# The output projection of a hybrid mLSTM/S5 block as seven block products instead of a full product, with its weight differences built on the way

## The chip, the cores and the metric

The kernel runs on one core of one Trainium2 chip. The metric is the device time of one execution in microseconds; lower is better.

## The reference

A decoder block on x of 1024 x 1024 (sequence by width) in float32. What matters here is its frame and its end:

```python
xn = rmsnorm(x, norm_pre_g)
u_a, z_a, o_a, i_a, f_a, u_b, z_b, g_pre = split(xn @ w_in)
y_a = mlstm_branch(u_a, z_a, o_a, i_a + b_i, f_a + b_f, ...) @ w_a_out   # 4 heads, chunks of 128
y_b = s5_branch(u_b, z_b, ...) @ w_b_out                                 # width 512
g = sigmoid(g_pre)                                                       # 2048 gates per row
merged = g[:, :1024] * y_a + g[:, 1024:] * y_b
out = x + rmsnorm(merged @ w_o, norm_post_g)                             # w_o is 1024 x 1024
```

## The kernel before, in words

**Arithmetic.** Every float32 matrix product is made of three matmuls. `dot3` (L181 to L184) multiplies high half by high half (L182), high by low (L183) and low by high (L184). So each operand is split first: the high half is a copy on ScalarE (L142 for weights), the low half is the difference to it on VectorE or GpSimd (L144 for weights). Helper `tt` (L505) is an elementwise operation of VectorE; many rows bear its line.

**Engines and queues.** The program order is the order of each engine; nothing is reordered. Every DMA, load or store, is issued on SyncE's queue (SP in the profile) in program order, and where a DMA has to wait (for data, for a buffer, for an earlier DMA), SyncE waits and all later DMAs stand behind it. `store` (L82) puts a store on the list `pending`, and `tick`, which `run` calls ahead of every unit of work, issues what stands there. `run` also issues the loads of the next `look[0]` units ahead. Matmul results go to PSUM: three banks named `pp` and five named `pm`.

**Weights.** A plan (L231 to L254) lists weight tiles in order of use. `take` and `pump` load the raw tile `wr` (L124) and split it into `wh` and `wl` some time ahead; `wp` has two buffers of each.

**Stages.** Norm and transposes of x; the gates (written to DRAM as `t1_d` and `t2_d`); the S5 branch; then the stage around the change, "the yb stage": first 8 units of the gated unit `glu_unit`, then 16 of `yb_unit`, which make the gated y_b. Unit n of these 16 multiplies 4 row tiles of K by 512 columns (12 matmuls) into the next of the five `pm` banks; VectorE (L844) combines the bank with a gate tile `aux` (128x512, six buffers, loaded from `t2_d` at L820 three units ahead, as `look[0]` is 3), and the result goes to `gb_d`, 256 KB, at the next tick. Then the four mLSTM heads follow. They start with `o_unit`, one for each of the 8 row tiles: 24 matmuls into the next of the three `pp` banks, 264 columns wide for the first head since the 8 gate columns i and f come along. VectorE adds the bias tile `bif` to these 8 (`gall`, L505), which together with ScalarE's read frees the bank. `bif` is loaded by two small DMAs, L879 and L880, which stand in SyncE's order behind the last `gb_d` store of the yb stage. After the heads comes the merge: `mg_unit` multiplies the last K tiles of `w_a_out`, applies the gates, adds the part of y_b and splits the result to `mh` (ScalarE, L1439) and `ml` (GpSimd, L1440).

**Output projection.** `wo_unit` (L1445 on) runs over 4 blocks of 256 columns and 8 row tiles: 8 tiles of K times 3 matmuls of 256 columns. ScalarE squares the bank with a running sum (L1460), VectorE multiplies it by the norm's gains `gpo`. In the last block GpSimd makes the row's factor `fs` from the sums (L1467, L1468), and `finish` (L1474) multiplies two halves by it, adds x and stores them.

Of the kernel before, what the change touches and what calls it, by code (L numbers as in the profile page):

```python
# [36 lines left out]
def hybrid_block(ctx, tc, x, norm_pre_g, w_in, conv_w, conv_b, w_q, w_k, w_v, b_i, b_f, head_g,  # L37
# [799 lines left out]
    def yb_unit(i, m, hf):  # L837
        if m == 0 and hf == 0:
            cur["yb"] = take(("yb", i))
        ct = 4 * i + m  # L840
# [3 lines left out]
        V.scalar_tensor_tensor(t2, t2, 1.0, o, op0=ALU.add, op1=ALU.mult)  # L844
# [570 lines left out]
    mh, ml = {}, {}

    def mg_pre(ct, hf):
        rs = slice(ct * P, (ct + 1) * P)
# [4 lines left out]
        maux[ct, hf] = (t1, pr, None)

    def mg_unit(ct, hf):
        if "ya3" not in cur:
# [12 lines left out]
        A.activation(mh[ct, hf], t1, AF.Copy)  # L1439
        defer(lambda: PL.tensor_tensor(ml[ct, hf], t1, mh[ct, hf].bitcast(F32), op=ALU.subtract))  # L1440
# [4 lines left out]
    def wo_unit(i, t):  # L1445
        if t == 0:
            cur["wo", i] = take(("wo", i), i > 0)
        if i == 0:
# [11 lines left out]
        A.activation(jk, o[:, :256], AF.Square, scale=1.0 / 32.0, accum_out=sso[:, t, i:i + 1])  # L1460
# [4 lines left out]
        if i == 3:
            s = fp.tile([P, 1], F32, tag="fs", bufs=4, name="fs")
            PL.tensor_tensor(s, sso[:, t, 3:4], sso[:, t, 4:5], op=ALU.add)  # L1467
            PL.tensor_tensor(s, s, halfm[:, 0:1], op=ALU.pow)  # L1468
# [74 lines left out]
```

## Time and profile before

| | us |
|---|---|
| median of 3 runs (lowest to highest) | 987.84 (987.65 to 988.62) |
| profiled execution, whole | 987.63 |
| its span in the profile | 985.9 |
| TensorE busy (5644 matmuls) | 972.8 |
| VectorE, ScalarE, GpSimd busy | 621.9, 352.9, 207.1 |
| the 16 units of the yb stage on TensorE | 339.6 to 383.2 |
| the output projection's last matmul starts at | 979.6 |

The span is what the profiler saw from the first to the last instruction; the execution's own time is 1.7 us longer. Rows of the timeline give start, length, engine, line, operation, output and inputs, shapes and, in brackets, how long the engine had stood still and who released it. PE is TensorE's matmuls, DVE is VectorE, ACT ScalarE, POOL GpSimd, SPq the DMAs that SyncE issues. A matmul's stated length (0.39 us for 512 columns) is longer than the distance to the next one (0.23 us), as they overlap. The granted clock is 0.999 over the span.

### The profile page before, as it was taken

To read this page: it belongs to the slowest core of one execution; us is meant where nothing else is said; L and a number is where in the kernel's file an instruction comes from. 1 tells how busy PE (TensorE), PEld (TensorE's weight loads), DVE (VectorE), ACT (ScalarE), POOL (GpSimd) and SP (SyncE) were. 2 spreads that over 40 slices of the span, in tenths; PEclk is the share of its full clock that TensorE was granted. 3 is DMA by queue.
4 is the path that set the end of the run, shared out by engine and by line. 5 is a ranking of instruction groups with operands and counts; after the bars stand their busy time and mean duration, and the time that the engine had idled before them with its cause. 6 is when DMAs were issued, how large, how long until landed. Compare 5 with 4: busy or idle time off the path is not lost.

```text
span 985.9 us, 15233 instructions
## 1 busy us (share of the span) xinstructions
PE 972.8 (99%) x5644; PEld 840.9 (85%) x5644; DVE 621.9 (63%) x1397; ACT 352.9 (36%) x697; POOL 207.1 (21%) x215
## 2 busy tenths in 40 slices
PE   9999999999999999999999999998999999999997
PEld 7888888888887889978998898888988888879997
DVE  5437968879644752444686677747775888664225
ACT  7413132231314421224544445434543452233211
POOL 3013122111112000013111321223222311462002
PEclk9999999999999999999999999999999999999999
DMA  7454323423434566115344254335437895772504
GB/s 257 109 159 150 96 89 99 111 57 110 110 97 166 186 216 229 59 68 148 97 134 152 82 178 124 134 97 177 133 117 226 281 302 191 243 249 90 193 1 172
DMA packets 113722, 145.17 MB, mean 147 GB/s; under 512 B 18888, under 2 KB 71280, under 8 KB 113648
## 3 DMA queue, kind: packets, MB, share of 16 engines
q1 hardware_dynamic: 113648, 144.21, 46.0%
q8 instruction: 44, 0.72, 0.3%
q14 instruction: 30, 0.25, 0.1%
HBM read 98.79 MB, written 45.38 MB: 146 GB/s over the span
## 4 chain that ended last, share of the span: by engine, by line
PE 88%; issue 3%; POOL 3%; DVE 2%; DMA 2%; ACT 1%; SPq 0%; DVEq 0%; POOLq 0%; ACTq 0%
PE pp L182 24%; PE pp L183 23%; PE pp L184 23%; PE pm L184 4%; PE pm L182 4%; PE pm L183 4%; PE pm L1151 1%; POOL wl L144 1%; PE pm L727 1%; PE pm L768 1%; PE pm L767 1%; PE pm L1074 1%; DMA so_d<-sow 1%; POOL ml L1440 1%; POOL t2k L1270 1%
## 5 line engine op out<-in xcount | busy, mean ns | idle before, releaser
L182 PE MATMUL pp<-xh,wh 128*128 128x512 f32 x768 | 306.9, 400 | 0.0
L183 PE MATMUL pp<-xl,wh 128*128 128x512 f32 x768 | 303.8, 396 | 0.0
L184 PE MATMUL pp<-xh,wl 128*128 128x512 f32 x768 | 303.8, 396 | 0.0
L182 PEld LDWEIGHTS pp<-xh,wh 128*128 128x128 f32 x768 | 144.4, 188 | 35.1 <-ACT wt L691 0.8
L184 PEld LDWEIGHTS pp<-xh,wl 128*128 128x128 f32 x768 | 144.4, 188 | 34.6
L183 PEld LDWEIGHTS pp<-xl,wh 128*128 128x128 f32 x768 | 144.5, 188 | 32.4 <-DVE xl L295 0.3
L144 POOL TENSOR_TENSOR wl<-wr,wh 128x1024 fp32r<-128x1024 f32 (+1 forms) x25 | 61.6, 2482 | 229.1 <-ACT wh L142 229.1
L142 ACT ACTIVATE wh<-wr 128x1024 fp32r<-128x1024 f32 (+2 forms) x74 | 71.0, 1006 | 46.5 <-PE pm L183 30.6
L184 PE MATMUL pp<-wh,ml 128*128 128x256 f32 x256 | 72.6, 284 | 1.3 <-POOL ml L1440 1.3
L144 DVE TENSOR_TENSOR wl<-wr,wh 128x1024 fp32r<-128x1024 f32 (+2 forms) x49 | 55.9, 1172 | 27.7 <-ACT wh L142 23.2
L182 PE MATMUL pp<-wh,xh 128*128 128x256 f32 (+1 forms) x256 | 72.3, 282 | 0.6 <-ACT sow L902 0.6
L183 PE MATMUL pp<-wl,mh 128*128 128x256 f32 x256 | 72.5, 283 | 0.0
L182 PE MATMUL pp<-wh,mh 128*128 128x256 f32 x256 | 71.9, 281 | 0.0
L184 PE MATMUL pp<-wh,xl 128*128 128x256 f32 (+1 forms) x256 | 71.8, 281 | 0.0
L183 PE MATMUL pp<-wl,xh 128*128 128x256 f32 (+1 forms) x256 | 71.8, 280 | 0.0
L308 ACT ACTIVATE tg<-pp 128x512 f32<-128x512 f32 x32 | 19.2, 598 | 127.4 <-PE pp L184 89.4
L1048 POOL TENSOR_TENSOR hll<-t2k,hlh 128x512 fp32r<-128x512 f32 x16 | 21.1, 1319 | 182.7 <-ACT hlh L1047 106.0
L184 PEld LDWEIGHTS pp<-wh,ml 128*128 128x128 f32 x256 | 48.1, 188 | 1.7 <-POOL ml L1440 1.7
L182 PEld LDWEIGHTS pp<-wh,mh 128*128 128x128 f32 x256 | 48.7, 190 | 0.5 <-ACT mh L1439 0.4
L182 PEld LDWEIGHTS pp<-wh,xh 128*128 128x128 f32 x256 | 48.1, 188 | 1.2 <-ACT sow L902 1.0
L183 PEld LDWEIGHTS pp<-wl,xh 128*128 128x128 f32 x256 | 48.2, 188 | 0.2
L184 PEld LDWEIGHTS pp<-wh,xl 128*128 128x128 f32 x256 | 48.1, 188 | 0.0
(412 smaller groups left out, 1810.0 us busy)
## 6 DMA issues: line engine op xcount, KB each, us to landing
wr<-in_w_in_dram SPq DMA_DIRECT2D x48, 512.0 KB
t_d<-tg SPq DMA_DIRECT2D x32, 256.0 KB
xt<-in_x_dram SPq DMA_DIRECT2D x8, 512.0 KB
aux<-t_d SPq DMA_DIRECT2D x16, 256.0 KB
gb_d<-aux SPq DMA_DIRECT2D x16, 256.0 KB
so_d<-sow SPq DMA_DIRECT2D x32, 128.0 KB
sz_d<-t2k SPq DMA_DIRECT2D x16, 256.0 KB
cs_d<-t2k SPq DMA_DIRECT2D x16, 256.0 KB
```

The source lines that it names most:

```text
L142: A.activation(hi, raw, AF.Copy)
L144: eng.tensor_tensor(wl[:, k0:k0 + n, c0:c0 + w], raw, hi.bitcast(F32), op=ALU.subtract)
L182: PE.matmul(o, lh, rh, start=first, stop=False)
L183: PE.matmul(o, lh, rl, start=False, stop=False)
L184: PE.matmul(o, ll, rh, start=False, stop=last)
L308: A.activation(t, o, AF.Tanh, scale=0.5)
L727: PE.matmul(o[NS * b2:NS * (b2 + 1), g * P:(g + 1) * P], q["wt"][:, ri, g, NS * b2:NS * (b2 + 1)], ut[b][:, 2 * g + b2, :], start=True, st ...
L767: PE.matmul(o, m0[:, 2 * g + b2, :], ut[b][:, 2 * g + b2, :], start=True, stop=False)
L768: PE.matmul(o, vs[:, b2, g].rearrange("p t n -> p (t n)"), ss_[:, b2, g, :], start=False, stop=True)
L1048: PL.tensor_tensor(lo, acc, hi.bitcast(F32), op=ALU.subtract)
L1074: PE.matmul(pm[:, 256 * k:256 * k + 256], wt[:, e, 256 + P * k:256 + P * k + P], wt[:, e, 0:256], start=e == 0, stop=e == 1)
L1151: PE.matmul(sc[:, :P], k_[:, m, sl], q_[:, m, sl], start=m == 0, stop=m == 1)
```

## The change

The product of `merged` (rows in two halves, K in two halves) and `w_o` (four blocks of 512 x 512) is written as seven products of 512 x 512 blocks, in the form of Strassen and Winograd, in place of eight. They run in the order p1, p2, p6, p5, p7, p4, p3. Each has four units (a row tile of 128 each, 4 tiles of K, 512 columns, 12 matmuls) that go into `pm` banks; the last unit of p3 is made in two halves of 256 columns.

- **Weight differences.** Four of the seven weights are differences of w_o's blocks. They are built during the yb stage: `wo_load` fetches an eighth of w_o (`wc`, two DMAs of 256 KB, rows of 1 KB) in the yb units 1, 2, 3, 4, 6, 8, 10 and 12; in the unit behind it `wo_comb` makes four subtractions of 128x256 on GpSimd and puts two stores of 256 KB to the new DRAM scratch `wt_d` on the list, which the next tick issues. The weights are loaded from there when their turn comes.
- **Sums of merged.** The merge units run in another order and write into blocks; the low halves are now made on VectorE. For each pair of row tiles `s_pair` makes two differences on VectorE and a sum on GpSimd, and GpSimd later makes one more difference (`split_s`, n = 4); each of the four results is split like any operand.
- **Second weights.** p2's weights are split into buffers of their own (`wset2`), which x's tiles `xh4` to `xl5` have left.
- **After each product** VectorE adds the bank to a block (`m1`, `u2` or `u4`); ScalarE squares the sum from SBUF rather than from PSUM; GpSimd multiplies by the gains (VectorE in p3). `finish` of row tile t stands behind the next unit (`defer`), but that of the last tile, 3, is called at once, and so comes ahead of that of tile 2.

The core of the diff:

```diff
+    wt_d = dscr.tile([2, 2, 512, 512], F32, name="wt_d")
...
-    for i in range(4):
-        plan(("wo", i), [w_o[0][:, 256 * i:256 * i + 256]], KT, 256)
+    wo11, wo12 = w_o[0][0:512, 0:512], w_o[0][0:512, 512:1024]
+    wo21, wo22 = w_o[0][512:1024, 0:512], w_o[0][512:1024, 512:1024]
+    for n, src in (("p1", wo11), ("p2", wo21), ("p6", wt_d[1, 1]), ("p5", wt_d[0, 0]), ("p7", wt_d[0, 1]),
+                   ("p4", wt_d[1, 0]), ("p3", wo22)):
+        plan(n, [src], 4, 512)
...
+    wsteps = deque((j, q) for j in range(4) for q in range(2))
+    wcomb = deque()
+    def wo_load():
+        j, q = wsteps.popleft()
+        n = 2 * j + q
+        t = gq.tile([P, 2, 2, DH], F32, tag=f"yg{n % 4}", name="wc")
+        rows = w_o[0].rearrange("(a j p) c -> j p a c", a=2, j=4)[j]
+        for a in range(2):
+            SY.dma_start(t[:, a], rows[:, a].rearrange("p (b c) -> p b c", b=2)[:, :, DH * q:DH * q + DH])
+        wcomb.append((j, q, t))
+    def wo_comb():
+        if wcomb:
+            j, q, t = wcomb.popleft()
+            sub_ = lambda o, a, b: PL.tensor_tensor(o, a, b, op=ALU.subtract)
+            b11, b12, b21, b22 = t[:, 0, 0], t[:, 0, 1], t[:, 1, 0], t[:, 1, 1]
+            sub_(b11, b12, b11)
+            sub_(b12, b22, b12)
+            sub_(b22, b22, b11)
+            sub_(b21, b21, b22)
+            for a in range(2):
+                store(wt_d[a][:, P * j:P * j + P, DH * q:DH * q + DH].rearrange("b p c -> p b c"), t[:, a])
...
         t2 = aux.pop((1, ct, hf))
+        wo_comb()
+        if (n := 8 * i + 4 * hf + m) in (1, 2, 3, 4, 6, 8, 10, 12):
+            wo_load()
         o = mbank()
         proj_cm(o, cur["yb"], m * P, ybh, ybl, HS[hf])
         V.scalar_tensor_tensor(t2, t2, 1.0, o, op0=ALU.add, op1=ALU.mult)
...
-        mh[ct, hf] = fp.tile([P, 512], F32R, name=f"mh{ct}{hf}")
-        ml[ct, hf] = fp.tile([P, 512], F32R, name=f"ml{ct}{hf}")
-        A.activation(mh[ct, hf], t1, AF.Copy)
-        defer(lambda: PL.tensor_tensor(ml[ct, hf], t1, mh[ct, hf].bitcast(F32), op=ALU.subtract))
...
-    def wo_unit(i, t):
...
-        hf = t // 4
-        sl = slice((t % 4) * P, (t % 4 + 1) * P)
-        o = bank()
-        proj_tm(o[:, :256], lambda k: mh[k, hf][:, sl], lambda k: ml[k, hf][:, sl], cur["wo", i], 0, 256,
-                KT)
-        cs = slice(256 * i, 256 * (i + 1))
-        jk = fp.tile([P, 256], F32, tag="fjk", bufs=1, name="fjk")
-        A.activation(jk, o[:, :256], AF.Square, scale=1.0 / 32.0, accum_out=sso[:, t, i:i + 1])
-        mul(ob[t][:, cs], o[:, :256], gpo[:, cs])
...
+        b, j = 2 * hf + ct // 4, ct % 4
+        if b != 2:
+            A.activation(ah[b][:, j], t1, AF.Copy)
+            defer(lambda: tt(al[b][:, j], t1, ah[b][:, j].bitcast(F32), ALU.subtract))
+        if hf:
+            pair.setdefault(j, []).append(ct)
+            if len(pair[j]) == 2:
+                defer(lambda: s_pair(j))
...
+    def s_pair(j):
+        a11, a12, a21, a22 = mrow(j, 0), mrow(4 + j, 0), mrow(j, 1), mrow(4 + j, 1)
+        tt(a21, a11, a21, ALU.subtract)
+        tt(a22, a22, a21, ALU.subtract)
+        PL.tensor_tensor(a11, a11, a22, op=ALU.add)
+        defer(split_1(2, j, a22, V))
+        for n, r in ((1, a11), (3, a21), (4, a12)):
+            late_s[n].append((j, r))
...
+    def mul_unit(w, lhs, o, tq, cs=slice(0, 512)):
+        hi, lo = lhs
+        sl = slice(tq * P, (tq + 1) * P)
+        for k in range(4):
+            dot3(o, hi[k][:, sl], lo[k][:, sl], *wcur[w](k, cs), k, k == 0, k == 3)
...
+    def wset2():
+        fetch()
+        key, _, _, raws = raw_q.popleft()
+        assert key == "p2"
+        h_ = [main.tile([P, 2, 512], F32R, tag=f"xh{4 + k}", name=f"w2h{k}") for k in range(2)]
+        l_ = [main.tile([P, 2, 512], F32R, tag=f"xl{4 + k}", name=f"w2l{k}") for k in range(2)]
+        for i in range(2):
+            raw = raws[i][2]
+            A.activation(h_[i], raw, AF.Copy)
+            V.tensor_tensor(l_[i], raw, h_[i].bitcast(F32), op=ALU.subtract)
+        wcur[2] = lambda k, cs: (h_[k // 2][:, k % 2, cs], l_[k // 2][:, k % 2, cs])
+        pending.append(fetch)
...
+    def p2(q):
...
+        mul_unit(2, (rows4(ah[1]), rows4(al[1])), o, q)
+        tt(cb_[0][q], cb_["m1"][:, q], o, ALU.add)
+        square(cb_[0][q], q, 0)
...
+    def p6(q):
+        if q == 0:
+            wset(6)
+            cb_["u2"] = block("a3", "u2")
+            y_space(4, 4)
+        o = mbank()
+        mul_unit(6, sv[2], o, q)
+        tt(cb_["u2"][:, q], cb_["m1"][:, q], o, ALU.add)
+        if q == 0:
+            pump()
+        if q < 2:
+            split_s(1, PL)
+        split_s(3, V)
...
+    def p3(q):
+        if q == 0:
+            wset(3)
+            cb_[1] = rows4(block("a7", "c12"))
+            cb_["raw"] = block("a6", "c12r")
+        n = 1 if q < 3 else 2
+        w = 512 // n
+        o = mbank()
+        for i in range(n):
+            cs = slice(w * i, w * i + w)
+            mul_unit(3, sv[4], o[:, cs], q, cs)
+            r = cb_["raw"][:, q, cs]
+            tt(r, cb_["u4"][:, q, cs], o[:, cs], ALU.add)
+            square(r, q, 1 + i)
+            mul(cb_[1][q][:, cs], r, cb_["g"][:, 512 + w * i:512 + w * i + w])
+            if i < n - 1:
+                tt(sso[:, q, 3:4], sso[:, q, 3:4], sso[:, q, 1:2], ALU.add)
+        s = rms(q, n)
+        if q < 3:
+            defer(lambda: finish(q, s))
+        else:
+            finish(q, s)
...
+    go(p1, 0)
+    fill(2)
+    for q in range(1, 4):
+        go(p1, q)
+        fill(1)
+        if q == 1:
+            wset2()
+    go(p2, 0)
+    fill(1)
+    pump()
+    for f, q in [(p2, q) for q in range(1, 4)] + [(f, q) for f in (p6, p5, p7, p4, p3) for q in range(4)]:
+        go(f, q)
+    flush2()
     tick()
```

SyncE at the start of the yb units, before: rows name the line, the DMA's destination and source, and its shape.

```order
L124 DMA wr<-in_w_in_dram 128x4x8
L82 DMA gb_d<-aux 128x512
L820 DMA aux<-t_d 128x512
L82 DMA gb_d<-aux 128x512
L820 DMA aux<-t_d 128x512
```

The same place after, where L83 is the store helper, L824 the gate tile's load and L838 `wo_load`:

```order
L83 DMA gb_d<-aux 128x512
L824 DMA aux<-t_d 128x512
L838 DMA wc<-in_w_o_dram 128x2x256 x2
L83 DMA gb_d<-aux 128x512
L824 DMA aux<-t_d 128x512
L838 DMA wc<-in_w_o_dram 128x2x256 x2
L83 DMA wt_d<-wc 128x2x256 x2
L83 DMA gb_d<-aux 128x512
L824 DMA aux<-t_d 128x512
```

Each gate tile from the second on now has a piece's loads ahead of it, and from the third on the stores of the piece before as well.

SyncE at the end of the yb units, before, from the last gate tiles to the bias loads of the first `o_unit`:

```order
L82 DMA gb_d<-aux 128x512
L820 DMA aux<-t_d 128x512
L82 DMA gb_d<-aux 128x512 x4
L879 DMA bif<-in_b_i_dram 128x4
L880 DMA bif<-in_b_f_dram 128x4
L124 DMA wr<-in_w_in_dram 128x4x256 x2
```

The same place after, where L912 and L913 load the bias:

```order
L83 DMA wt_d<-wc 128x2x256 x2
L83 DMA gb_d<-aux 128x512
L824 DMA aux<-t_d 128x512
L838 DMA wc<-in_w_o_dram 128x2x256 x2
L83 DMA gb_d<-aux 128x512
L83 DMA wt_d<-wc 128x2x256 x2
L83 DMA gb_d<-aux 128x512 x3
L912 DMA bif<-in_b_i_dram 128x4
L913 DMA bif<-in_b_f_dram 128x4
```

The bias loads now stand behind the stores of all eight pieces.

VectorE at the end of the program, before: the last two units' products with the gains and the two halves of each `finish`.

```order
L505 TENSOR_TENSOR ob_9171<-pp,gpo 128x256
L1474 SCALAR_TENSOR_TENSOR ob_9171<-ob_9171,fs,xr_9172 128x512 x2
L505 TENSOR_TENSOR ob_9201<-pp,gpo 128x256
L1474 SCALAR_TENSOR_TENSOR ob_9201<-ob_9201,fs,xr_9202 128x512 x2
```

The same place after. `c12r` is the sum of `u4` and the bank, `c_9559` its product with the gains; L1560 is `finish`, with `xr_9450` for row tile 1, `xr_9452` for tile 3 and `xr_9451` for tile 2.

```order
L509 TENSOR_TENSOR c12r<-u_9270,pm 128x512
L509 TENSOR_TENSOR c_9559<-c12r,gpo 128x512
L1560 SCALAR_TENSOR_TENSOR c_9087<-c_9087,fs,xr_9450 128x512
L1560 SCALAR_TENSOR_TENSOR c_9559<-c_9559,fs,xr_9450 128x512
L509 TENSOR_TENSOR c12r<-u_9270,pm 128x256
L509 TENSOR_TENSOR c_9559<-c12r,gpo 128x256
L509 TENSOR_TENSOR sso<-sso 128x1
L509 TENSOR_TENSOR c12r<-u_9270,pm 128x256
L509 TENSOR_TENSOR c_9559<-c12r,gpo 128x256
L1560 SCALAR_TENSOR_TENSOR c_9088<-c_9088,fs,xr_9452 128x512
L1560 SCALAR_TENSOR_TENSOR c_9559<-c_9559,fs,xr_9452 128x512
L1560 SCALAR_TENSOR_TENSOR c_9088<-c_9088,fs,xr_9451 128x512
```

Row tile 1's `finish` stands ahead of the sum that reads the first half of the last unit's bank, and tile 2's behind tile 3's.

More of the change, by code (lines that the diff above doesn't have):

```diff
@@ L1493, in hybrid_block, with load_res, wset @@
-    n_hf = len(fillers) - n_ya
-    for ct in range(2, 6):
-        mgf(ct, 1)
+            V.scalar_tensor_tensor(c, c, s, xres[t][:, qs_], op0=ALU.mult, op1=ALU.add)
+            store(out[0, t * P:(t + 1) * P, qs_], c)
+    def load_res(t, tag):
+        xres[t] = main.tile([P, D], F32, tag=tag, name=f"xr{t}")
+        store(xres[t], x[0, t * P:(t + 1) * P, :])
+    rows4 = lambda a: [a[:, k] for k in range(4)]
+    def wset(n):
+        wh, wl = take(f"p{n}", False)
+        wcur[n] = lambda k, cs: (wh[:, k, cs], wl[:, k, cs])
@@ new lines, in pmul, with p1 @@
+    def pmul(dst, a, g0):
+        n = a.shape[1]
+        PL.tensor_tensor(dst, a, cb_["g"][:, g0:g0 + n], op=ALU.mult)
+    def p1(q):
+        if q == 0:
+            wset(1)
+            cb_["m1"] = block("a9", "m1")
+        o = mbank()
+        mul_unit(1, (rows4(ah[0]), rows4(al[0])), o, q)
+        A.copy(cb_["m1"][:, q], o)
+    def p2(q):
+        if q == 0:
+            c11 = [main.tile([P, 2, 512], F32, tag=f"xh{6 + i}", name=f"c11{i}") for i in range(2)]
+            cb_[0] = [c11[i // 2][:, i % 2] for i in range(4)]
+            hl1 = [block("a1", "s1h", F32R), block("a2", "s1l", F32R)]
+            sv[1] = [rows4(a) for a in hl1]
+        o = mbank()
+        mul_unit(2, (rows4(ah[1]), rows4(al[1])), o, q)
+        tt(cb_[0][q], cb_["m1"][:, q], o, ALU.add)
+        square(cb_[0][q], q, 0)
+        if q == 1:
+            cb_["g"] = main.tile([P, D], F32, tag="xl6", name="gpo")
+            store(cb_["g"], norm_post_g[0].partition_broadcast(P))
+        if q > 1:
+            split_s(1, PL)
@@ new lines, in p7, with p4 @@
+    def p7(q):
+        if q == 0:
+            wset(7)
+            cb_[3] = rows4(block("a1", "c22"))
+        o = mbank()
+        mul_unit(7, sv[3], o, q)
+        c, t = cb_[3][q], 4 + q
+        tt(c, cb_["u4"][:, q], o, ALU.add)
+        tt(cb_["u2"][:, q], cb_["u2"][:, q], o, ALU.add)
+        square(c, t, 1)
+        pmul(c, c, 512)
+        if q == 0:
+            pump()
+        V.tensor_scalar(sso[:, t, 3:4], sso[:, t, 1:2], 4.0 * EPS, None, op0=ALU.add)
+    def p4(q):
+        if q == 0:
+            wset(4)
+            cb_[2] = rows4(block("a5", "c21"))
+            for t, tag in zip(range(4), ("xh2", "xh3", "xl2", "xl3")):
+                load_res(t, tag)
+        o = mbank()
+        mul_unit(4, (rows4(ah[3]), rows4(al[3])), o, q)
+        c = cb_[2][q]
+        tt(c, cb_["u2"][:, q], o, ALU.add)
+        square(c, 4 + q, 0)
+        pmul(c, c, 0)
+        s = rms(4 + q, 0)
+        defer(lambda: finish(4 + q, s))
+        V.tensor_scalar(sso[:, q, 3:4], sso[:, q, 0:1], 4.0 * EPS, None, op0=ALU.add)
+        if q == 0:
+            pump()
```

143 lines of the change are left out of this document (86 added, 57 removed).

## The prediction

> **What bounds the kernel now.** First the page: its busy line and its chain.
>
> ```profile
> PE 972.8 (99%) x5644; PEld 840.9 (85%) x5644; DVE 621.9 (63%) x1397; ACT 352.9 (36%) x697; POOL 207.1 (21%) x215
> PE 88%; issue 3%; POOL 3%; DVE 2%; DMA 2%; ACT 1%; SPq 0%; DVEq 0%; POOLq 0%; ACTq 0%
> ```
>
> TensorE is busy for 99% of the span and carries 88% of the chain. So fewer matmul columns shorten the kernel, and any wait given to TensorE lengthens it. Next, what keeps close behind TensorE where the change adds DMAs: the yb stage in windows (columns: sum of time, TensorE, weight loads, VectorE, ScalarE, GpSimd busy, granted clock, DMA share, GB/s), then two lines of its DMA view, the first of them the rate in 40 slices of 350 to 385 us.
>
> ```profile
> 340.00:350.00 10.00, 10.00 (x46) 8.29 (x45) 7.54 (x10) 4.43 (x7) 1.71 (x5) 1.00 0.13 44
> 350.00:360.00 10.00, 10.00 (x46) 8.29 (x45) 5.03 (x7) 0.52 (x1) 0.00 (x0) 1.00 0.80 254
> 360.00:370.00 10.00, 10.00 (x45) 8.28 (x45) 5.83 (x8) 2.06 (x2) 0.00 (x0) 1.00 0.90 286
> 370.00:380.00 10.00, 10.00 (x46) 8.27 (x45) 2.52 (x4) 0.00 (x0) 0.00 (x0) 1.00 0.94 318
> 390.00:400.00 10.00, 10.00 (x85) 10.00 (x84) 0.52 (x3) 1.16 (x3) 0.00 (x0) 1.00 0.24 85
> ...
> GB/s 0 0 80 301 319 321 240 366 339 407 377 377 269 274 274 246 295 405 337 356 220 153 260 259 286 303 383 405 384 295 253 323 290 302 368 178 96 213 0 42
> DMA packets 7076, 9.27 MB, mean 265 GB/s; under 512 B 1552, under 2 KB 3600, under 8 KB 7074
> ```
>
> GpSimd has nothing to do there, but DMA is at 80 to 94% from 350 us on, against 13% before and 24% behind. I take 310 GB/s for what it carries when it has work (the middle of the slices; 407 the best, 265 the mean with gaps). How close it runs to TensorE the queues tell:
>
> ```profile
> 350.85 2.06 SPq L124 DMA_DIRECT2D wr<-in_w_in_dram  x4
> 376.68 0.32 SPq L820 DMA_DIRECT2D aux<-t_d  x1
> 384.44 0.43 SPq L879 DMA_DIRECT2D bif<-in_b_i_dram  x1
> 384.92 0.46 SPq L880 DMA_DIRECT2D bif<-in_b_f_dram  x1
> ...
> 358.83 0.69 DVE L844 SCALAR_TENSOR_TENSOR aux<-aux,pm 128x512 f32<-128x512 f32 x1 [4.49 <-DMA aux<-t_d]
> 383.37 0.69 DVE L844 SCALAR_TENSOR_TENSOR aux<-aux,pm 128x512 f32<-128x512 f32 x1 [2.03 <-PE pm L184]
> 387.74 0.18 DVE L505 TENSOR_TENSOR gall<-pp,bif 128x8 f32<-128x8 f32 x1 [1.14 <-DMA bif<-in_b_f_dram]
> ...
> 383.17 0.28 PE L182 MATMUL pp<-wh,xh 128*128 128x264 f32 x1
> 391.86 0.29 PE L182 MATMUL pp<-wh,xh 128*128 128x264 f32 x1
> ```
>
> VectorE waits 4.49 us for a gate tile already in yb unit 4, with TensorE covered by its five banks. The last gate tile leaves at 376.68, seven microseconds ahead of its use at 383.37. The fourth o_unit (391.86; the first starts at 383.17) needs the bank that the first frees, and that needs the bias: sum at 387.74. So TensorE has 391.86 − 387.74 = 4.1 us to spare there.
>
> **Part by part. (1) Columns.** A 256-wide unit of 24 matmuls, and the pitch at 512:
>
> ```profile
> 902.72 0.42 DVE L505 TENSOR_TENSOR ob<-pp,gpo 128x256 f32<-128x256 f32 x1 [2.12 <-ACT fjk L1460]
> 934.40 0.42 DVE L505 TENSOR_TENSOR ob<-pp,gpo 128x256 f32<-128x256 f32 x1 [2.46 <-ACT fjk L1460]
> ...
> 847.01 0.39 PE L182 MATMUL pp<-xh,wh 128*128 128x512 f32 x1
> 871.51 0.40 PE L182 MATMUL pp<-xh,wh 128*128 128x512 f32 x1
> ```
>
> Eleven units lie between the first two rows, 2.88 us each; 32 make 92.2. Between the other two lie 105 matmuls, 0.2333 us each; 28 units of 12 make 78.4. The saving is 13.8 us.
>
> **(2) Low halves.** They leave GpSimd, and with them this wait: −1.3 us.
>
> ```profile
> PE pp L184 <- POOL ml L1440: 1.3, 2, 1.1
> 651.25 2.60 POOL L1124 TENSOR_TENSOR q<-hlh,hll 128x512 f32<-128x512 f32 x2
> ```
>
> **(3) The weight differences.** Eight pieces of 0.52 MB loaded and 0.52 MB stored add 8.39 MB to a stage with 9.27. Each store makes SyncE wait for the loads' landing and for GpSimd's sums; behind it stand the next gate tile, which VectorE needs to free TensorE's bank, and at the end the bias. GpSimd's sums of 256 columns take, by the second row, an estimated 0.7 us each. I follow the queue on before's clock:
> - Gate tile 4 is in hand at 358.8. Piece 0's loads stand next, 0.52 MB at 310 GB/s: 360.5. Two sums hide behind the second load, two follow: its stores leave at about 362.
> - As far as piece 3 the next loads are issued ahead of a piece's stores, so only bytes count: gb_d, aux, wc and wt_d are 1.57 MB, 5.1 us a piece. Piece 3's stores leave at 362 + 15.3 = 377.3.
> - From piece 4 on a piece's loads come behind the previous stores and a gb_d and aux pair. Each piece then costs its bytes, 5.1, the time from issue to use of its last load, some 2.7 (the bias, issued at 384.92, is used at 387.74), and two sums, 1.4: 9.2 us. Four of them: piece 7's stores leave at 414.
> - The bias follows behind those stores and four gb_d, 1.57 MB and the way from issue to use: 414 + 5.1 + 2.7 = 421.8. The fourth o_unit starts at about 422 where it stood at 391.86.
>
> That is +30 us. The five banks of yb cost TensorE some of it earlier, but the time isn't paid twice: o_units 0 to 2 fill in only once. Lower end: were only bytes to count and the rate the best slice's, 8.39 / 0.407 = 20.6, less 2.9 us of DMA idle in the last five slices (mean 106 of 310 over 4.4 us) and the 4.1 to spare: 14. Upper end: at the mean of 265 GB/s a piece's bytes take 5.9 us, and with the bias that is 0.8 × 8 ≈ 7 more: 37. I take 30, whose parts have rows. By the Trainium skill (DMA: Bandwidth & Descriptors, "Anatomy of one DMA") a DMA takes about 2.0 us plus its bytes at 436 GB/s; the sum by that would be an estimated 3.6 us for each early piece and 7.0 for each late one, and the jam about 15. No slice here reaches that rate.
>
> **(4) A cold TensorE.** It will stand still for over 20 us in (3). What a TensorE that comes from rest loses shows at the program's start:
>
> ```profile
> 1.42 0.90 PE L376 MATMUL pp<-ident 128*128 128x128 f32 x3 [1.42 <-POOL halfm L77]
> 4.46 0.58 PE L376 MATMUL pp<-ident 128*128 128x128 f32 x3
> 5.32 0.49 PE L376 MATMUL pp<-ident 128*128 128x128 f32 x3
> 7.17 0.38 PE L376 MATMUL pm<-ident 128*128 128x128 f32 x2
> ```
>
> The first 14 transposes take 3.04 us, 0.217 each; the 17 from 5.32 to 7.17 take 0.109 each: 14 × 0.108 = 1.5 us more. Range 0 to 1.5; I take 1.5.
>
> **(5) Start of product 6, and the last unit.** The rows: a sum with GpSimd busy and one without, GpSimd's stretch, the splits of a weight tile.
>
> ```profile
> 864.03 1.08 DVE L505 TENSOR_TENSOR ft<-ft,fpa 128x512 f32<-128x512 f32 x1
> 887.25 0.69 DVE L505 TENSOR_TENSOR ft<-ft,fpa 128x512 f32<-128x512 f32 x1
> ...
> 862.82 6.39 POOL L1440 TENSOR_TENSOR ml<-ft,mh 128x512 fp32r<-128x512 f32 x4 [1.29 <-ACT mh L1439]
> ...
> 897.91 2.36 DVE L144 TENSOR_TENSOR wl<-wr,wh 128x1024 fp32r<-128x1024 f32 x2 [0.52 <-ACT wh L142]
> ```
>
> Product 6 needs the low halves of S2, whose last block hangs on the last merge unit. Behind that unit VectorE has two merge steps, the split of p6's weights (2.36), the sum of p2's second unit, a low half, the two differences, the sum of p2's third unit and the low half itself: 8 × 0.69 + 2.36 = 7.9 us, with hand-overs an estimated 8.8, and 10.7 if five of them take 1.08 as beside a busy GpSimd. TensorE has three units of p2 meanwhile, 3 × 2.8 = 8.4. GpSimd makes sums and S1's low halves just there, so I take +2.3 (range 0.5 to 4).
>
> Other sums, splits and gains of the seven products are two to four VectorE operations a unit, at most 4 × 0.69 beside 2.8 of matmuls: hidden, at 0, unless every one is slowed to 1.08 (4.3 a unit, rival C).
>
> In the last unit the second half writes the bank that the first half's sum must have read. That sum stands behind tile 2's sum and gains and tile 1's finish: 4 × 0.69 + 0.42 = 3.2 us after the third unit, plus 0.3 of hand-over, against 1.44 of matmuls: +2.0 (0.5 to 2.5).
>
> **(6) The tail.**
>
> ```profile
> 979.60 0.28 PE L184 MATMUL pp<-wh,ml 128*128 128x256 f32 x1
> 980.48 0.42 DVE L505 TENSOR_TENSOR ob<-pp,gpo 128x256 f32<-128x256 f32 x1 [0.57 <-ACT fjk L1460]
> 981.37 1.42 DVE L1474 SCALAR_TENSOR_TENSOR ob<-ob,fs,xr 128x512 f32<-128x512 f32 x2 [0.47 <-POOL fs L1468]
> ```
>
> A sum of 0.42 now stands ahead of the square, and tile 2's finish, 1.42, behind tile 3's: +1.85.
>
> Sum against the profiled execution's own 987.63 (0.21 below the median of the three runs, so it stands for them): 987.63 − 13.8 − 1.3 + 30 + 1.5 + 2.3 + 2.0 + 1.85 = 1010.2, forecast 1010.
>
> **Rivals.**
> - **A, hidden traffic (faster).** If SyncE's queue never comes late, terms 3 and 4 vanish: 987.63 − 13.8 − 1.3 + 2.3 + 2.0 + 1.85 = 978.7. For it: five banks ahead, and a last gate tile seven microseconds early. It decides by whether the bias lands within the 4.1 us to spare; against it, VectorE waits for gate tiles already, and 8.39 MB are 27 us at 310 GB/s. Chance 0.11; a small jam of 5 to 12 us, 984 to 992, has 0.06.
> - **B, bytes alone.** If the waits for landing and sums overlap with other transfers, the jam is 27.1 − 2.9 − 4.1 = 20: 1000. For it: the DMA rate counts in the first four pieces as it stands. Against it: from piece 4 on nothing is queued behind the waiting store. Chance 0.20.
> - **C, more waits.** The jam at its upper end of 37, or the sums of the products slowed by GpSimd: a unit of four then takes 4.3 us instead of 2.8, and five to seven such units give +7 to +10. That is 1017 to 1020. Against the second: GpSimd has only one or two operations of 1.3 us in a unit of 2.8. Chance 0.10.
> - The forecast has 0.53.
>
> **How the numbers follow.** A measurement of this kernel can tell about 0.2%, 2 us. Faster by more: A and a third of the small jam, 0.13. Within: the middle of the small jam, 0.04. Slower: the rest, 0.83. The range leaves out A and the small jam (0.17) and reaches from B's lower part to C: 996 to 1020.
>
> **Right or wrong.** In the profile after, the chain should run through wc, wt_d and bif on SyncE; VectorE's `gall` sum should stand near 421, idle before it, and the fourth o_unit near 422; the stores of wt_d from the fifth on should lie about 9 us apart. TensorE's waits should show S2's low half once and VectorE before the last twelve matmuls. I am wrong on the main term if the fourth o_unit starts before 406 (bytes at the best rate), and altogether if at 392.

## The result, and the profile after

| | before | after |
|---|---|---|
| median, us (4 runs each, on one chip) | 988.01 (987.65 to 988.62) | 1016.76 (1014.59 to 1018.08) |
| profiled execution, us | 987.63 | 1016.37 |
| its span, us | 985.9 | 1014.6 |
| TensorE busy, us | 972.8 | 965.1 |

The ratio after to before is 1.0288, 95% interval 1.0269 to 1.0307: the change makes the kernel 2.9% slower. The profiled executions differ by 28.7 us. First the page's busy line and its chain, after.

```profile
PE 965.1 (95%) x5224; PEld 817.3 (81%) x5224; DVE 664.7 (66%) x1430; ACT 364.1 (36%) x689; POOL 250.2 (25%) x255
PE 49%; DMA 6%; DVE 5%; POOL 4%; issue 2%; SPq 1%; ACT 1%; DVEq 0%; POOLq 0%; ACTq 0%
```

TensorE has 420 matmuls fewer and carries only 49% of the chain, where it had 88%. What it waits for tells the rest: the view of TensorE's waits (total, times, longest).

```profile
PE pp L183 <- DVE gall L509: 22.3, 1, 22.3
PE pm L183 <- DVE aux L877: 5.7, 3, 2.8
PE pm L183 <- DVE c12r L509: 5.2, 1, 5.2
PE pm L183 <- ACT s2h L1512: 2.5, 1, 2.5
...
PE pm L185 <- DVE s2l L1513: 0.5, 1, 0.5
```

None of the five stands in before's view. The first is the fourth o_unit's wait, right behind the yb stage, the second lies in the yb stage, the third in the last unit, the other two at product 6. SyncE's timeline shows the jam itself, the stores of pieces 4 to 7 and the bias:

```profile
386.38 1.99 SPq L83 DMA_DIRECT2D wt_d<-wc  x2
...
395.59 2.00 SPq L83 DMA_DIRECT2D wt_d<-wc  x2
...
405.00 1.97 SPq L83 DMA_DIRECT2D wt_d<-wc  x2
...
415.22 1.97 SPq L83 DMA_DIRECT2D wt_d<-wc  x2
...
419.25 0.45 SPq L913 DMA_DIRECT2D bif<-in_b_f_dram  x1
```

They leave 9.2, 9.4 and 10.2 us apart; the first of them comes 8.7 us behind piece 3's (377.71). Then VectorE's sum with the bias and TensorE's fourth o_unit, with five of its matmuls:

```profile
411.12 0.69 DVE L877 SCALAR_TENSOR_TENSOR aux<-aux,pm 128x512 f32<-128x512 f32 x1 [5.02 <-DMA aux<-t_d]
...
422.41 0.24 DVE L509 TENSOR_TENSOR gall<-pp,bif 128x8 f32<-128x8 f32 x2 [7.80 <-DMA bif<-in_b_f_dram]
```

```profile
422.64 0.59 PE L183 MATMUL pp<-wh,xh 128*128 128x264 f32 x1 [22.27 <-DVE gall L509]
423.02 0.42 PE L184 MATMUL pp<-wl,xh 128*128 128x264 f32 x1
...
425.44 0.40 PE L183 MATMUL pp<-wh,xh 128*128 128x264 f32 x1
...
426.05 0.28 PE L184 MATMUL pp<-wl,xh 128*128 128x264 f32 x1
...
428.49 0.28 PE L183 MATMUL pp<-wh,xh 128*128 128x264 f32 x1
```

The fourth o_unit starts at 422.64 where it stood at 391.86: 30.8 us late. Behind the pause 11 steps take 2.42 us, 0.22 each; from 426.05 on 20 steps take 2.44, 0.122 each. Further on the distance to before is 32.2 us, so the slow matmuls cost 1.4. The windows show the same as the granted clock (the column behind the engines), in this pause and in two others, at product 6 and in the last unit:

```profile
410.00:420.00 10.00, 0.00 (x0) 0.00 (x0) 3.49 (x3) 0.00 (x0) 5.27 (x9) 0.50 0.55 198
...
940.00:950.00 10.00, 6.99 (x23) 5.01 (x22) 7.04 (x10) 7.53 (x15) 5.07 (x4) 0.83 0.45 156
...
1000.00:1014.00 14.00, 2.93 (x12) 2.63 (x12) 7.84 (x15) 1.74 (x6) 3.29 (x6) 0.59 0.40 150
```

The seven products' own pace, from a matmul of product 6 behind its waits to the last of p3's third unit, 209 steps on:

```profile
949.13 0.39 PE L183 MATMUL pm<-wh,s2h 128*128 128x512 f32 x1
...
996.78 0.39 PE L185 MATMUL pm<-wh,s4l 128*128 128x512 f32 x1
```

That is 0.228 us each. At last the end, TensorE and then VectorE:

```profile
998.30 0.28 PE L185 MATMUL pm<-wh,s4l 128*128 128x256 f32 x1
1003.77 0.58 PE L183 MATMUL pm<-wh,s4h 128*128 128x256 f32 x1 [5.19 <-DVE c12r L509]
...
1006.28 0.41 PE L185 MATMUL pm<-wh,s4l 128*128 128x256 f32 x1
```

```profile
1000.65 0.68 DVE L509 TENSOR_TENSOR c12r<-u,pm 128x512 f32<-128x512 f32 x1
...
1001.98 1.41 DVE L1560 SCALAR_TENSOR_TENSOR c<-c,fs,xr 128x512 f32<-128x512 f32 x2
1003.30 0.41 DVE L509 TENSOR_TENSOR c12r<-u,pm 128x256 f32<-128x256 f32 x1
...
1008.69 2.74 DVE L1560 SCALAR_TENSOR_TENSOR c<-c,fs,xr 128x512 f32<-128x512 f32 x4 [1.08 <-POOL fs L1553]
```

The third unit of p3 has its last matmul at 996.78, but VectorE comes to its sum only at 1000.65.

### The profile page after: what moved, and what is told of

It is laid out like the page before. It is cut to its first block, busy times and chain, and to the rows that moved or that the text cites. A ratio compares the mean times of both kernels' runs of the same rounds, so it can differ in the third digit from the quotient of the medians.

```text
span 1014.6 us, 14528 instructions
## 1 busy us (share of the span) xinstructions
PE 965.1 (95%) x5224; PEld 817.3 (81%) x5224; DVE 664.7 (66%) x1430; ACT 364.1 (36%) x689; POOL 250.2 (25%) x255
## 4 chain that ended last, share of the span: by engine, by line
PE 49%; DMA 6%; DVE 5%; POOL 4%; issue 2%; SPq 1%; ACT 1%; DVEq 0%; POOLq 0%; ACTq 0%
PE pp L183 11%; PE pp L184 11%; PE pp L185 11%; PE pm L185 4%; PE pm L183 4%; PE pm L184 4%; DMA wc<-in_w_o_dram 3%; POOL wc L844 2%; DMA wr<-in_w_in_dram 1%; PE pm L1184 1%; DVE tg L862 1%; DVE c L1560 1%; PE pm L1107 1%; DMA so_d<-sow 1%; SPq L83 1%
## 5 line engine op out<-in xcount | busy, mean ns | idle before, releaser
L183 PE MATMUL pp<-xh,wh 128*128 128x512 f32 x736 | 293.9, 399 | 0.0
L184 PE MATMUL pp<-xl,wh 128*128 128x512 f32 x736 | 291.0, 395 | 0.0
L185 PE MATMUL pp<-xh,wl 128*128 128x512 f32 x736 | 290.9, 395 | 0.0
L185 PEld LDWEIGHTS pp<-xh,wl 128*128 128x128 f32 x736 | 138.2, 188 | 33.2
L183 PE MATMUL pp<-wh,xh 128*128 128x256 f32 (+1 forms) x256 | 73.1, 285 | 22.9 <-DVE gall L509 22.3
L145 DVE TENSOR_TENSOR wl<-wr,wh 128x1024 fp32r<-128x1024 f32 (+2 forms) x53 | 64.7, 1251 | 27.2 <-ACT wh L143 22.6
L844 POOL TENSOR_TENSOR wc<-wc 128x256 f32<-128x256 f32 x32 | 26.6, 834 | 75.1 <-issue 45.0
L877 DVE SCALAR_TENSOR_TENSOR aux<-aux,pm 128x512 f32<-128x512 f32 x16 | 10.7, 685 | 46.3 <-DMA aux<-t_d 46.3
L1061 DVE SCALAR_TENSOR_TENSOR t2k<-pp,par,t2k 128x511 f32<-128x511 f32 (+2 forms) x48 | 35.7, 744 | 5.1 <-ACT t2k L1054 4.6
L1237 ACT ACTIVATE cth<-ct 128x516 fp32r<-128x516 f32 x28 | 17.8, 637 | 53.2 <-DVE ct L1227 51.0
L1157 POOL TENSOR_TENSOR q<-hlh,hll 128x512 f32<-128x512 f32 x16 | 21.9, 1390 | 49.6 <-DVE q L509 39.5
```

Source lines behind the costliest of these rows:

```text
L145: eng.tensor_tensor(wl[:, k0:k0 + n, c0:c0 + w], raw, hi.bitcast(F32), op=ALU.subtract)
L183: PE.matmul(o, lh, rh, start=first, stop=False)
L184: PE.matmul(o, lh, rl, start=False, stop=False)
L185: PE.matmul(o, ll, rh, start=False, stop=last)
L844: sub_ = lambda o, a, b: PL.tensor_tensor(o, a, b, op=ALU.subtract)
L1061: V.scalar_tensor_tensor(acc[:, s:], o[:, :512 - s], cw[:, j, ct:ct + 1], acc[:, s:], op0=ALU.mult, op1=ALU.add)
```

## The experiments

The theory after the result: the jam is made by stores that wait on SyncE, ahead of everything that TensorE needs, and the two waits near the end by VectorE's queue. Rivals: the bytes alone; the rest of the change; the bank, or GpSimd's factors. Times without an interval are single ones, good to some 2 us; the places in the trace say more.

### The jam

**no_diff.** The products without their weight differences.

```diff
-        wo_comb()
-        if (n := 8 * i + 4 * hf + m) in (1, 2, 3, 4, 6, 8, 10, 12):
-            wo_load()
...
-    for n, src in (("p1", wo11), ("p2", wo21), ("p6", wt_d[1, 1]), ("p5", wt_d[0, 0]), ("p7", wt_d[0, 1]),
-                   ("p4", wt_d[1, 0]), ("p3", wo22)):
+    for n, src in (("p1", wo11), ("p2", wo21), ("p6", wo11), ("p5", wo12), ("p7", wo21),
+                   ("p4", wo22), ("p3", wo22)):
...
```

> Loads, sums and stores of the weight differences are left out; the four products read plain blocks of w_o, so their weights are not the differences. Theory: 1016.4 - 30.8 - 1.4 = 984, the fourth o_unit at 392. It tells what the seven products cost by themselves: by the forecast's terms 979, with the measured waits at product 6 and in the last unit about 984. Rival (part of the 32 us comes from the rest of the change): above 990.

Measured 984.23, with the fourth o_unit here:

```profile
391.84 0.29 PE L182 MATMUL pp<-wh,xh 128*128 128x264 f32 x1
```

So the whole 32 us come with the weight differences. The seven products by themselves are worth 3.4 us against before's profiled execution (one execution each), with the waits at product 6 and in the last unit still in them. TensorE waits at product 6 exactly as in after, 2.5 and 0.5 us, and yet no slow clock follows. The window around it, with the granted clock behind the engines, 1.00:

```profile
910.00:920.00 10.00, 6.99 (x30) 5.20 (x29) 8.29 (x11) 7.93 (x16) 5.51 (x4) 1.00 0.45 160
```

In its place no_diff has 3.4 us at half clock from 686.7 on, behind a wait of 2.05 us for `ksl` (a tile of the mLSTM heads), a wait that before and after have too, 2.12 and 1.99 us, without a slow clock.

**late_stores.** The same bytes in the same stage, each piece's stores one unit later.

```diff
...
+        while wlate:
+            store(*wlate.popleft())
         wo_comb()
...
-                store(wt_d[a][:, P * j:P * j + P, DH * q:DH * q + DH].rearrange("b p c -> p b c"), t[:, a])
+                wlate.append((wt_d[a][:, P * j:P * j + P, DH * q:DH * q + DH].rearrange("b p c -> p b c"), t[:, a]))
```

> All bytes stay in the yb stage; only each piece's two stores are put one yb unit later, so that the loads have landed and the sums are made when SyncE comes to them. Theory (the store that waits on SyncE, with nothing queued behind it, is what costs): the jam shrinks to about what the bytes take, fourth o_unit at 406 to 412, time 1000 to 1006. Rival (bytes alone, at a lower rate than I took): nothing changes, fourth o_unit at 422, time 1016.

Measured 1000.58. TensorE's fourth o_unit; then SyncE's waits for the sums and the loads from 350 to 425 us, in after (two lines) and in this run:

```profile
407.39 0.59 PE L183 MATMUL pp<-wh,xh 128*128 128x264 f32 x1 [15.63 <-DVE gall L509]
```

```profile
SPq L83 <- POOL wc L844: 21.4, 14, 3.4
SPq L83 <- DMA wc<-in_w_o_dram: 7.1, 5, 2.3
...
SPq L83 <- POOL wc L845: 8.1, 8, 3.4
```

The jam falls from 30.8 to 15.5 us with not a byte less. SyncE's waits at the stores fall from 28.5 us to 9.1 (8.1 for the sums and 1.0 for loads). They are not gone: the stores of the last piece still wait over 4 us. So half of the jam, at the least, was SyncE standing at a store; how much of the other half is bytes, and how much the waits that are left, this run doesn't part.

**no_sums.** The yb stage without GpSimd's work.

```diff
-            sub_(b11, b12, b11)
-            sub_(b12, b22, b12)
-            sub_(b22, b22, b11)
-            sub_(b21, b21, b22)
```

> As after, in the yb stage, but GpSimd's subtractions are left out: the stores write plain blocks of w_o, so the four weights are not the differences. Bytes and order of the DMAs are the same. Theory (GpSimd's sums lie in the chain from a late piece's loads to its stores, with 2.4 to 3.1 us each): four late pieces get shorter by that, the fourth o_unit starts at 410 to 413 instead of 422.6, time 1004 to 1007. Rival (the sums hide behind the transfers): 422 and 1016.

Measured 1002.96, a little under the range expected:

```profile
409.34 0.59 PE L183 MATMUL pp<-wh,xh 128*128 128x264 f32 x1 [12.77 <-DVE gall L509]
```

GpSimd's sums account for 13.3 of the 30.8 us, though GpSimd itself is idle most of the stage: they lie in the chain from load to store. This isn't a second part beside late_stores' 15.3 us: the sums are most of what the stores wait for. Of the 13.3 us 5.5 are there when piece 3's stores leave (372.19 here, 377.71 in after); the four late pieces, 7.7 us apart here and 9.4 in after, give 1.6 to 1.7 us each, and 1.2 come behind the last.

**bias_early.** The two loads of the bias are issued ahead of the yb stage.

```diff
+    bif = main.tile([P, 8], F32, name="bif")
+    SY.dma_start(bif[:, 0:4], b_i[0].partition_broadcast(P))
+    SY.dma_start(bif[:, 4:8], b_f[0].partition_broadcast(P))
     gl = ExitStack()
...
```

> Only the two bias loads are taken to the front of the yb stage; all pieces stay. Theory: the fourth o_unit no longer waits for the bias behind the last stores, but still for VectorE, which has the last yb unit at 411.1 and a weight split to 414.6: fourth o_unit at 415, and then so_d's stores behind the last wt_d may cost up to 3 us: 1008.5 to 1012. Rival (the bias is not what holds TensorE; the banks of yb are): no change, 1016.

Measured 1020.31, outside the range expected, though the fourth o_unit starts close to where it was expected. TensorE, then ScalarE, then SyncE:

```profile
416.14 0.59 PE L183 MATMUL pp<-wh,xh 128*128 128x264 f32 x1 [14.17 <-DVE gall L509]
427.70 0.59 PE L183 MATMUL pp<-wh,xh 128*128 128x264 f32 x1 [3.81 <-DVE gall L509]
```

```profile
427.06 0.69 ACT L935 ACTIVATE sow<-pp 128x256 f32<-128x256 f32 x2 [25.11 <-DMA so_d<-sow]
```

```profile
421.66 18.46 SPq L83 DMA_DIRECT2D so_d<-sow  x8
```

The next o_units need the two `sow` buffers, whose stores `so_d` stand behind the same `wt_d` stores. What the bias gives, the next transfer in SyncE's order takes back; in this run the whole stage also came 1.8 us later, as VectorE's weight split ahead of the yb sums stood at 351.50 instead of 349.68. Behind the o_units this run is only 0.5 us later than after, so within the stage the early bias gave back 1.3 us of 30.8. Of the 3.9 us that it takes longer than after the other 3.4 come later: 1.5 with 3.4 us at half clock at 720, behind the wait for `ksl`, the rest bit by bit, without a cause that is shown. What the early bias shows is read from the stage: the bias was only the one that came last in the jam, not its cause.

**spread.** The pieces go to 24 gate units of the S5 stage, in one buffer there.

```diff
     def g_unit(i, m, hf):
+        n = 4 * (i - 1) + 2 * hf + m
+        if n % 3 == 0 and wsteps:
+            wo_load()
+        if n % 3 == 1:
+            wo_comb()
...
```

> The same eight pieces, sums and stores, but taken out of the yb stage and spread over 24 gate units of the S5 stage: loads in one unit, sums in the next, stores at the tick behind that, so that no store waits on SyncE. Theory (SyncE's queue in the yb stage makes the jam): the fourth o_unit starts at about 392 again, not at 422.6; of the 1016.4 us go the 30.8 us of the jam and the 1.4 us of cold TensorE behind it: 984. Rival (8.39 MB cost their time wherever they stand): the stage that takes them gets longer by 5 to 20 us, 990 to 1004. Both leave the waits at product 6 and in the last unit as they are.

Measured 989.90 median, ratio to before 1.0022 (1.0012 to 1.0032). The jam in the yb stage is gone, but 5.7 us over no_diff stay, just under the rival's range. In the S5 stage TensorE waits for VectorE:

```profile
251.26 0.41 PE L733 MATMUL pm<-v_r,bd_r 128*32 128x128 f32 x2 [1.42 <-DVE v_r L538]
253.39 0.42 PE L733 MATMUL pm<-v_n,bd_i 128*32 128x128 f32 x1 [1.72 <-DVE ec_i L704]
```

With the slow clock behind it (252.1 to 258.9) this place accounts for 6.1 us of delay against no_diff. VectorE was busy for 213.8 of the 270 us from 60 to 330, and for 197.1 in no_diff, with the same work. Operation by operation some 12 us of this lie beside GpSimd's sums. The rest comes of VectorE's being late: its long operations now meet GpSimd's split of a weight, where short ones stood in no_diff. So it is at the wait for `v_r`, VectorE and then GpSimd:

```profile
245.42 2.95 DVE L538 TENSOR_TENSOR tv<-ct_t,pw_i 128x576 f32<-128x576 f32 x1
...
245.06 5.53 POOL L145 TENSOR_TENSOR wl<-wr,wh 128x1024 fp32r<-128x1024 f32 x2 [2.10 <-ACT wh L143]
```

Such an operation takes 0.75 us alone. SyncE still waits 11.3 us for the sums in this stage, but none of TensorE's waits there is for a DMA. That the same bytes can cost next to nothing outside the yb stage is shown by the last run below.

**heads.** The pieces go to the o_units and the units behind them. In `piece(u)` an even u loads, an odd one makes the sums, and stores are listed a unit later.

```diff
-    for f in os_:
-        run(unit(f))
+    for u, f in enumerate(os_):
+        run(unit(f, lambda u=u: piece(u)))
...
```

> The pieces leave the yb stage for the 8 o_units and the 11 units behind them at the start of the heads: a piece's loads every second unit, its sums in the next, its stores a unit later, in the four buffers that the attention doesn't use yet. There DMA was at 24%, GpSimd idle and VectorE nearly so. Theory (place and waiting make the cost, not the bytes): the fourth o_unit at 392, no wait of TensorE there, time 984, as without any differences. Rival (what the pieces cost when spread over the S5 stage, 5.7 us, is their bytes): 989 to 991 here too.

Measured 987.87 median, ratio 0.9991 (0.9977 to 1.0005): no wait at the fourth o_unit, but 3.6 us over no_diff, between theory and rival. TensorE waits at the gates now, 1.3 and 1.2 us, and falls 2.9 us behind no_diff there. (The profiled execution, 989.78, is one of the longer ones; 1.7 us of its distance to no_diff are a slow clock at product 6.) VectorE and GpSimd at the gates:

```profile
416.64 0.19 DVE L509 TENSOR_TENSOR g_pl<-g_pl,g_z 128x32 f32<-128x32 f32 x1
...
417.08 0.73 DVE L509 TENSOR_TENSOR g_pl<-g_pl,g_z 128x32 f32<-128x32 f32 x1
```

```profile
417.03 2.38 POOL L915 TENSOR_TENSOR cz<-cz 128x256 f32<-128x256 f32 x3 [0.91 <-DMA wt_d<-cz]
```

An operation of 32 columns takes 0.73 instead of 0.19 us when it meets a GpSimd sum of 0.8, as if it waited for the rest of that instruction, which ends at 417.82. The Trainium skill (SBUF: State Buffer, "Who interferes with whom") says so as a rule: the port pair that VectorE and GpSimd share is held by one of them for a full instruction. The trace agrees.

### Product 6 and the last unit

**p6_pool.** The low halves of product 6's weights are made on GpSimd.

```diff
     go(p2, 0)
     fill(1)
+    lo_pool[0] = True
     pump()
+    lo_pool[0] = False
```

> The low halves of product 6's weights go from VectorE to GpSimd; all else as after, the jam too. Theory (VectorE's queue behind the last merge unit makes product 6 wait): 2.36 us leave that queue, so the wait falls from 2.5 + 0.5 to under 1 us, and the slow clock behind it, 1.7 us, is not started: 1016.4 - 2.4 - 1.7 = 1012.3. Rival (the wait comes from the merge's loads or from ScalarE): product 6 waits as before.

Measured 1016.04; in this run the jam was 1 us longer (23.3 for 22.3). TensorE's waits at product 6, and the pair of differences ahead of it, on VectorE, in this run and after:

```profile
PE pm L185 <- DVE s2l L1513: 1.4, 1, 1.4
...
PE pm L183 <- ACT s2h L1512: 0.4, 1, 0.4
```

```profile
939.36 3.49 DVE L509 TENSOR_TENSOR r<-r,r 128x512 f32<-128x512 f32 x2
```

```profile
941.09 1.41 DVE L509 TENSOR_TENSOR r<-r,r 128x512 f32<-128x512 f32 x2
```

The wait falls from 3.0 to 1.8 us, not below 1: of the 2.36 us that left VectorE's queue 2.1 came back, as its differences meet GpSimd's split. No slow clock follows here, but that isn't shown to be the edit's doing: in no_diff none follows the full wait of 2.5 and 0.5 us either. This run comes to product 6 2.1 us later than after, by its longer jam and by 3.4 us at half clock at 718.5, behind a wait of 1.8 us for `ksl`; so the whole time doesn't show what the edit gives.

**two_banks.** The last unit's second half gets a bank of its own (`o = mbank() if i else o`).

> The second half of the last unit goes into a PSUM bank of its own, so it need not wait for VectorE. Theory (VectorE is late at the end, the bank only shows it): TensorE's wait of 5.2 us and its slow clock there vanish, but VectorE's last sum moves only from 1006.7 to 1004.2, so the time falls by 2.5 us to 1014. Rival (the wait for the bank is the cost): it falls by 5.2 + 1.1 = 6.3 us to 1010.

Measured 1014.38. TensorE's wait is gone; VectorE's sums of the two halves:

```profile
1003.63 0.41 DVE L509 TENSOR_TENSOR c12r<-u,pm 128x256 f32<-128x256 f32 x1
...
1004.76 0.41 DVE L509 TENSOR_TENSOR c12r<-u,pm 128x256 f32<-128x256 f32 x1
```

The last sum moves from 1006.73 to 1004.76 and the time by 2.0 us (2.3 counted from the last unit, to which this run comes 0.3 us late), not by 6.3: the bank only showed that VectorE was late.

**gains_pool and defer2.** Why is it late? In the first the gains of three units go to GpSimd (`pmul` for `mul`), in the second the finishes of p4's tiles stand two units behind (`defer(..., 2)`).

> The multiplications by the gains of p3's first three units go from VectorE to GpSimd; the last unit's halves stay. Theory (VectorE carries 2.8 us a unit there and cannot catch up a delay that it brings along): 3 x 0.69 us leave its queue, TensorE's wait falls from 5.2 to about 3.1, too short for the slow clock: 1016.4 - 2.1 - 1.1 = 1013.2. Rival (VectorE waits for the factors from GpSimd, and more work there makes it later): the wait stays at 5.2 or grows.

> As after, but the finishes of p4's four row tiles stand two units behind their unit instead of one. Theory (VectorE comes late to the last unit because those finishes wait for GpSimd's factors, 1.3 and 0.7 us): the waits go, TensorE's wait of 5.2 us falls to about 3.2, too short for the slow clock: 1016.4 - 2.0 - 1.1 = 1013.3. Rival (VectorE is simply full there, and what is put off falls on p3): TensorE's wait stays or grows, 1016 to 1018.

Measured 1014.65 and 1014.60; TensorE's wait falls to 4.6 and 4.7 us, half a microsecond each, where about two were expected. The other 1.2 us by which both runs are shorter than after lie ahead of the edits. Two pairs of finishes in gains_pool, one in defer2 (VectorE):

```profile
996.94 1.84 DVE L1560 SCALAR_TENSOR_TENSOR c<-c,fs,xr 128x512 f32<-128x512 f32 x2
...
999.31 2.33 DVE L1560 SCALAR_TENSOR_TENSOR c<-c,fs,xr 128x512 f32<-128x512 f32 x2
```

```profile
989.01 2.44 DVE L1560 SCALAR_TENSOR_TENSOR c<-c,fs,xr 128x512 f32<-128x512 f32 x2
```

Such a pair takes 1.41 us alone. So the first gives back 0.43 + 0.92 of its 2.07 us. In the second the waits for factors are gone, but VectorE is then at work without a gap from 982.0 to 1002.4. Neither the gains nor the factors are the cause by themselves: VectorE is full through p4 and p3, the more so beside GpSimd. In after its queue begins to fall behind at the split of p3's weights (2.61 us from 983.24, after 1.68 us of waiting for ScalarE's copy), which puts its sum of p4's second unit at 985.77, some 2.4 us behind the unit's matmuls. No run moved that split; how the work would have to be cut to keep up there is left open.

### A version that beats both

**best.** Three pieces in the last third of the S5 stage, four in the o_units, one behind the gates; p6_pool, two_banks and defer2; tile 2's finish ahead of tile 3's.

```diff
+    def s5_piece(n):
+        if 23 <= n < 32:
+            piece(n % 3 == 2)
...
+        run(unit(f, lambda u=u: piece(u % 2 == 0)))
...
+        run(unit(f, lambda u=u: piece(u == 6)))
...
-        if q < 3:
+        if q < 2:
             defer(lambda: finish(q, s))
+        elif q == 2:
+            cb_["s2"] = s
         else:
+            finish(2, cb_["s2"])
             finish(q, s)
```

> The seven products with what the runs pointed to. Three pieces stand in the last third of the S5 stage, where VectorE is busy for about half the time, four in the o_units, one behind the gates' small operations; product 6's low halves of weights are made on GpSimd; the last unit's second half has a bank of its own; the finishes of p4's rows stand one unit later, and tile 2's finish stands ahead of tile 3's. Theory (place, queue order and VectorE's queue, not the products, made the change slow): 984.2 without differences, 0 to 2 for the pieces, less 2.4 to 2.9 at product 6, 2.0 for the bank, 1 to 2 for the finishes and 1.1 for their order: 976 to 980, faster than before by 8 to 12 us. Rival (the savings at the end are one and the same, VectorE's queue, and the pieces cost 3 to 4 as in the heads): 982 to 984.

Measured 980.36 median against 989.10, ratio 0.9912 (0.9898 to 0.9926): 0.9% faster than before, with its median 0.4 us over the range expected and its profiled execution, 978.50, within it. Its fourth o_unit starts at 391.82, TensorE's waits at product 6 are 0.4 and 1.4 us, and in the last unit there is none. VectorE's finishes of tile 2 and tile 3:

```profile
970.02 1.41 DVE L1573 SCALAR_TENSOR_TENSOR c<-c,fs,xr 128x512 f32<-128x512 f32 x2
971.87 1.41 DVE L1573 SCALAR_TENSOR_TENSOR c<-c,fs,xr 128x512 f32<-128x512 f32 x2 [0.44 <-POOL fs L1566]
```

Tile 2's now fills the time in which tile 3's factor is made. The 8.39 MB cost nothing in their new places: up to 687 us TensorE is nowhere later than in no_diff by more than 0.3 us. There no_diff falls to half clock for 3.4 us and this kernel doesn't, behind the same wait for `ksl`, 2.05 and 1.98 us. So 1.5 of the 5.7 us between the two profiled executions are not an effect of the edits; the edits at product 6 and at the end give about 4.2, less than the 6.5 to 8 that their prices summed to. In that the rival was right; in its price for the pieces it was not.

## Why the prediction was right, and where its sizes were off

The time, 1016.76, lies within 996 to 1020 and is slower as forecast, 6.8 us above the forecast of 1010. By its steps, in the profiled executions:

| term | forecast | measured | where |
|---|---|---|---|
| 1, 2 columns and low halves | −15.1 | about −16.9 | 28 x 12 x 0.228 = 76.6 instead of 78.4 |
| 3 the jam | +30 | +30.8 | fourth o_unit 391.86 to 422.64 |
| 4 cold TensorE behind it | +1.5 | +1.4 | distance to before further on 32.2 |
| 5 product 6 | +2.3 | +3.0, and 1.7 of slow clock | waits 2.5 + 0.5; half clock from 944.5 on for 3.4 us |
| 5 the last unit | +2.0 | +5.2, and 1.2 of slow clock | 12 matmuls 2.51 us (1003.77 to 1006.28) for 1.29 |
| 6 the tail | +1.85 | +2.0 | last matmul to the end 8.3 for 6.3 us |

The measured terms sum to 28.4 of the 28.7 us; the rest is in small waits.

- **The jam** was right in place and mechanism: SyncE's order, late pieces 8.7 to 10.2 us apart where I had 9.2, the bias as the last in the row. Its size came out partly by luck. Piece 3's stores left at 377.71, where I had 377.3, but I had counted only bytes up to there, 5.1 us a piece. Without the sums these pieces leave 4.1 us apart (359.96 to 372.19 in no_sums), which is an estimated 385 GB/s for 1.57 MB, not my 310; the sums, which I took as hidden, added 5.5 us. The two errors cancel. In the late pieces the parts hold: 7.7 us without the sums where I had 7.8, and 1.6 to 1.7 us of sums where I had 1.4.
- **The rivals to the jam.** Rival B, bytes alone, falls: the jam was 30.8 us and not 20, and the same bytes cost 15.5 when most of the waits at the stores are taken out. Rival A falls with the first row of the waits. The 15 us that the prediction works out from the Trainium skill's figure for one DMA are half of what was measured; that section gives its figure for DMAs that GpSimd issues, and SyncE issues all of these. The upper end was added up a little high: 0.8 × 8 is 6.4, not 7.
- **Product 6** had the queue that I named, but not the sizes in it. I had put five operations at 1.08 us; two were slowed (1.29 at 932.15 and 1.21 at 943.20), and in front of the weight split VectorE stood 1.65 us for ScalarE's copy, which I had left out. TensorE waited first for S2's high half (2.5 us), whose copy stands behind VectorE's two differences, and only then for the low half that I had named (0.5).
- **The last unit** is the step that was mis-sized. I counted from the third unit's end as if VectorE were free then ("4 × 0.69 + 0.42 = 3.2 us after the third unit"). It was 3.4 us behind: tile 2's sum began at 1000.65, and the unit ended at 997.0 with 0.3 for the hand-over. Rival C had a part of the reason, VectorE slowed by GpSimd (a finish of 2.45 instead of 1.41 us at 989.82), but I priced it as a longer unit and not as a delay that the last unit inherits; the units themselves kept their pace, 0.228 us a matmul. I had put the other work of the products at 0 as hidden; it was hidden from TensorE, and still filled VectorE.
- **The slow clock** was counted once and came four times: in the yb stage (384.7, 3.4 us, where it costs nothing of its own, as SyncE sets the time), in the jam, at product 6 and in the last unit. The last two cost 1.7 and 1.2 us that I had not counted. At product 6 it was chance: the same waits of 2.5 and 0.5 us bring it in after and not in no_diff.
- **The range** held partly by luck. Its upper end came from C's prices, 1017 to 1020, and neither of C's two cases came true as priced; they happened to cover the last unit's delay and the slow clocks.

## What to carry to other kernels

A store that waits for a computation holds up all later loads on its queue, so put it where its data has long been ready, or where nothing urgent stands behind it; what it costs is read from who stands behind it, one after the other, not from its bytes. Freeing one of those only shows the next: bias_early took the bias out of the row and gained 1.3 us of 30.8 in that stage, and nothing in the time. And before work goes to an idle GpSimd, look at what VectorE does at that moment: its operations took from one and a half to four times as long here, and a queue that is full carries the delay on to where it is paid. Where two variants differ by a few microseconds, look first where each was at half clock: here 1.7 us came and went with no change at the place.
